# A decoder layer on one core: the low parts of the input projections' weights made by ACT and an adding DMA instead of DVE

## The chip, the cores and the metric

The kernel runs on one core of one Trainium2 chip. Its engines are TensorE (PE in the rows, with PEld its weight loads), VectorE (DVE), ScalarE (ACT) and GpSimd (POOL); SyncE (SP) issues most of the transfers. The metric is device time in microseconds, the median over runs; a profiled execution of the kernel is read beside it.

## The reference

One layer of a hybrid decoder on 512 prompt tokens and 8 x 4 decode tokens, d_model 1024: a half-step SwiGLU block, a mixer, a second half-step SwiGLU block, a gated per-layer embedding, and a final RMSNorm. All is in fp32. The mixer is where the change lies:

```python
proj = (h @ w_in).astype(f32)          # h: normed x, one combined input projection
z, xbc, dt_raw, q, fr, iv, og = jnp.split(proj, points, axis=-1)
# xbc: short convolution of width 4, then SiLU, gives xs, B, C (1536 columns)
y, new_ssm = _ssd_chunked(xs, dt, a, bm, cm, ssm0)        # 16 Mamba-2 heads, chunks of 128
y = y + d_skip[:, None] * xs                               # then * silu(z), norm
f = lb + (1.0 - lb) * jax.nn.sigmoid(fr)
o, new_hg = _gla_chunked(silu(q), 1.0 - f, iv, log(f), hg0)  # 8 HGRN2 heads, chunks of 16
o = rmsnorm(o) * hg_norm * silu(og)
mixed = concatenate([y_ssd, o]) @ w_out
```

## The kernel before

**Tiling.** Activations are kept transposed, 128 partitions by 544 columns (512 prompt and 32 decode tokens), and are read in two halves of 272 columns. The matmuls of the dense projections keep nearly fp32 precision with a faster format: every fp32 weight and activation is split into a high part, rounded to fp32r, and a low part, which is the rest (value minus high part). `mm6` forms a product as hi·xhi + hi·xlo + lo·xhi: per block of 128 input rows six matmuls, the first two with (whi, xwh), the next two with (whi, xwl), and the last two with the low part of the weight, (wlo, xwh).

**One projection.** `proj(src)` (L745) makes 128 columns of the input projection. `slab(src)` (L132) loads 512 KB of weights into `wraw` (two buffers, issued by SP, L138), lets ACT round it into `whi` (`cp`, L81; three buffers) and DVE make `wlo` = wraw − whi (`tt`, L69; three buffers). Then PE runs 8 x 6 = 48 matmuls (L84) into `ps_in`. Since the order in a block is whi, whi, whi, whi, wlo, wlo, the fifth matmul is the first that reads `wlo`. `proj` is called 52 times: 12 times for the convolution's columns (the loop over m), 32 times for the four projections of each of the 8 HGRN2 heads (f, q, v, og), and 8 times for z, the last two of them after the heads. The 16 slabs of the output projection w_out and others also go through `slab`; they are loaded by the same three buffers.

**Stages.** The first SwiGLU block ends at about 392 us of the span, and the first matmul of an input projection starts at 392.67. The 12 convolution projections run to about 515 us; there one projection follows the other on PE. Then the heads: per head h the code calls v of head h, f and q of head h+1 and og of head h, and puts between them the head's small matmuls: `attend` (pairs of decays, L1070 and others), `outs` (state updates, the decode states L1100), `finish`, and the stages of one chunk of the Mamba heads (`ssd_chunk` by `unit()`: L896 transposes of `cT`, then L943 and L946, which make y from `E`, `xdt` and `yk`, and a DVE row L72 that adds them into `cT`). `ps_s` are the small PSUM buffers (four), `ps_in` the large (two). The gates of a head (L994, L995, two scans on DVE) come from f. A head takes some 36 us; the z projections and the tail follow until about 843 us.

**Order.** In this stage the code of before and of the change leaves the order on each engine to a scheduler that builds the program; each engine then runs its own list in order, and waits at a row for what it reads, or for a buffer to come free. A DMA issued by POOL or SP likewise stands in that engine's list.

Of the kernel before, what the change touches and what calls it, by code (L numbers as in the profile page):

```python
# [9 lines left out]
F32 = mybir.dt.float32  # L10
F32R = mybir.dt.float32r
BF16 = mybir.dt.bfloat16
AF = mybir.ActivationFunctionType
ALU = mybir.AluOpType
# [3 lines left out]
P = 128  # L18
# [30 lines left out]
def body(ctx, tc, xT, pT, hconv, hssm, hhg, vecs, csts, w1u, w1d, w_in, w_dt, w_o, w2u, w2d, w_pg, w_pp,  # L49
         y_o, conv_o, ssmp_o, hgp_o, ssms_o, hgs_o):  # L50
    nc = tc.nc
    V, A, G, PE = nc.vector, nc.scalar, nc.gpsimd, nc.tensor

    def after(ins, prev):
        if prev is not None:
            tc.add_manual_dep(ins.ins, prev.ins.name,
                              mybir.DependencyInfo(mybir.DependencyClass.NoSync, mybir.DependencyReason.DATA),
                              reason="issue order")
# [3 lines left out]
    def pin(ins):  # L62
        if pinned[0]:
            after(ins, chain.get(ins.ins.engine))
            chain[ins.ins.engine] = ins
        return ins

    def tt(out, a, b, op, eng=None):
        pin((eng or V).tensor_tensor(out=out, in0=a, in1=b, op=op))  # L69
# [10 lines left out]
    def cp(out, a):  # L80
        pin(A.copy(out, a))  # L81
# [6 lines left out]
    def act(out, in_, f, scale=1.0, bias=0.0, **kw):  # L88
        ins = pin(A.activation(out=out, in_=in_, func=f, scale=scale, bias=bias, **kw))  # L89
        if tabled[1] and f not in (AF.Copy, AF.Square):  # L90
            after(ins, tabled[0])
            tabled[0] = ins

    def f32(t):
        return t.bitcast(F32)
# [3 lines left out]
    wp = ctx.enter_context(tc.tile_pool(name="wp", bufs=3))  # L99
# [32 lines left out]
    def slab(src, n=KD, parts=1):  # L132
        raw = wp.tile([P, 8, P], F32, name="wraw", tag="wraw", bufs=2)
        hi = wp.tile([P, 8, P], F32R, name="whi", tag="whi")
        lo = wp.tile([P, 8, P], F32R, name="wlo", tag="wlo")
        for i in range(parts):
            s = slice(i * n // parts, (i + 1) * n // parts)
            nc.sync.dma_start(raw[:, s], src[:, s])  # L138
            cp(hi[:, s], raw[:, s])
            tt(lo[:, s], raw[:, s], f32(hi[:, s]), ALU.subtract)  # L140
        return hi, lo
# [6 lines left out]
    def mm6(ps, whi, wlo, xhi, xlo, start, stop, m=P):  # L148
        seq = ((whi, xhi), (whi, xlo), (wlo, xhi))
        for n, (w, x) in enumerate(seq):  # L150
            for hf in range(2):
                mm(ps[:m, hf, :HN], w, x[:, hf * HN:(hf + 1) * HN], start=start and n == 0,
                          stop=stop and n == 2)
# [586 lines left out]
    with tc.tile_pool(name="ma", bufs=20, reuse_waits="tile") as ap:  # L740
# [2 lines left out]
            return ap.tile([P, T], dt, name=nm, tag="a")  # L743

        def proj(src):  # L745
            hi, lo = slab(src)
            ps = big.tile([P, 2, 512], F32, name="ps_in", tag="big")
            for k in range(KD):
                mm6(ps, hi[:, k], lo[:, k], xw[k][0], xw[k][1], k == 0, k == KD - 1)
            return ps  # L750

        cT = [ring(f"cT{m}") for m in range(12)]
        with ExitStack() as mix:
# [87 lines left out]
            for m in range(12):  # L841
                ps = proj(w_in[m])
                if m in (1, 3, 6, 8):
                    next(dtg, None)
                cin = sp.tile([P, SO + 7 * NB], F32, name="cin", bufs=2)
                G.memset(cin[:, 0:3], 0.0)
                smp = cin[:, SO:].rearrange("p (b t) -> p b t", t=7)
                G.tensor_copy(smp[:, :, 0:3], hist[:, m].rearrange("p (b t) -> p b t", t=3))
                tt(cin[:, 3:3 + HN], ps[:, 0, :HN], r[:, :HN], ALU.mult)
                tt(cin[:, 3 + HN:SO], ps[:, 1, :TP - HN], r[:, HN:TP], ALU.mult)  # L850
                tt(smp[:, :, 3:7], ps[:, 1, TP - HN:HN].rearrange("p (b t) -> p b t", t=4),
                   r[:, TP:].rearrange("p (b t) -> p b t", t=4), ALU.mult)
                G.tensor_copy(ncv[:, m, 0:3], cin[:, SO - 3:SO])
                G.tensor_copy(ncv[:, m, 3:27].rearrange("p (b t) -> p b t", t=3), smp[:, :, 4:7])
                L = SO + 7 * NB - 3
                ca = sp.tile([P, SO + 7 * NB], F32, name="ca", bufs=2)
                ts(ca[:, :L], cin[:, 0:L], vc("conv_w", m), ALU.mult, vc("conv_b", m), ALU.add)
                for j in range(1, 4):
                    stt(ca[:, :L], cin[:, j:j + L], vc("conv_w", 12 * j + m), ca[:, :L], ALU.mult, ALU.add)
                act(cT[m][:, :TP], ca[:, :TP], AF.Silu)  # L860
                act(cT[m][:, TP:].rearrange("p (b t) -> p b t", t=4),
                    ca[:, SO:].rearrange("p (b t) -> p b t", t=7)[:, :, 0:4], AF.Silu)
# [107 lines left out]
            def ev(h, i, nm):  # L970
                ps = proj(w_in[20 + 4 * h + i])
                t = hp.tile([P, T], F32, name=nm, tag=nm, bufs=1)
                tt(h2(t), ps[:, :, :HN], h2(r), ALU.mult)
                return t

            def zv(m, nm):
                ps = proj(w_in[12 + m])
                t = hp.tile([P, T], F32, name=nm, tag=nm, bufs=1)
                tt(h2(t), ps[:, :, :HN], h2(r), ALU.mult)
                return t  # L980
# [198 lines left out]
        with tc.tile_pool(name="mx", bufs=1, reuse_waits="tile") as xp:  # L1179
            mo = []  # L1180
            for k in range(8):
                hi = xp.tile([P, T], F32R, name="ohh", tag="ohl", bufs=16)
                lo = xp.tile([P, T], F32R, name="ohl", tag="ohl", bufs=16)
# [36 lines left out]
            for i, (m, h) in enumerate(halves):  # L1220
# [3 lines left out]
                hi, lo = slab(w_o[m, :, 8 - 8 * h:16 - 8 * h])  # L1224
# [21 lines left out]
    with tc.tile_pool(name="f3", bufs=34, reuse_waits="tile") as fp:  # L1246
# [3 lines left out]
        def eslot(nm, dt=F32):  # L1250
            return fp.tile([P, T], dt, name=nm, tag="e", bufs=12)
# [3 lines left out]
        for k in range(2):  # L1255
            t = eslot("pt")
            nc.sync.dma_start(t, pT[k])
            hi, lo = eslot("pth", F32R), eslot("ptl", F32R)
# [3 lines left out]
        for m in range(KD):  # L1262
            hi, lo = wpp[m // 4]
# [67 lines left out]
        for hf in range(2):  # L1331
# [3 lines left out]
            for m in range(KD):  # L1335
                if hf == 0 and m >= 2:
                    gslab(m)
                hi, lo = wg[m]
# [135 lines left out]
```

## Time and profile before

| | us |
|---|---|
| median of 2 runs | 1418.51 (1417.12 to 1419.89) |
| the profiled execution | 1418.97 |
| its span | 1417.2 |
| PE busy, of the span | 1384.7 (98%) |
| DVE busy | 1000.6 (71%) |
| ACT busy | 684.3 (48%) |
| POOL busy | 268.8 (19%) |

The profiled execution's own time is 1.8 us above its span. The mean granted TensorE clock is 0.98 of full speed. Busy time says how long an engine ran instructions; whether it sets the end is read from the idle time of the engine that is full, PE, and from what released it. Times in the rows are us from the span's start.

### The profile page before, as it was taken

Reading aid. Unit: us, or ns where it says so; the run is one execution under the profiler, and the core shown is the slowest. Engines: PE = TensorE matmul, PEld = TensorE weight load, DVE = VectorE, ACT = ScalarE, POOL = GpSimd, SP = SyncE. Lnnn points to the kernel's source line nnn. Section 1 sums busy time; section 2 is a strip of 40 time slices with the busy share of each in tenths; the row PEclk is TensorE's granted clock in tenths of the full one; section 3 lists DMA queues with packets and bytes.
Section 4 is the critical chain, followed back from the end, with each engine's and each line's share of the span. In section 5 each row is a group of like instructions: output and inputs, shape, how many; then the busy total and the mean of one; then the engine's idle time right before and its main releaser. Section 6 shows DMA issues by size and latency. Waiting matters only on the chain.

```text
span 1417.2 us, 27123 instructions
## 1 busy us (share of the span) xinstructions
PE 1384.7 (98%) x11069; PEld 1342.9 (95%) x11069; DVE 1000.6 (71%) x1603; ACT 684.3 (48%) x1232; POOL 268.8 (19%) x245
## 2 busy tenths in 40 slices
PE   7999999999999999999999999999899999999997
PEld 7999999999999999999999799999899999999896
DVE  6696666666568887777776577566877777776465
ACT  6544444443444365555553375455444444443655
POOL 0133332232111100000001021101333333320200
PEclk9999999999999999999999999999999999999898
DMA  6133233332432422222222445551344443334311
GB/s 228 43 93 105 90 90 94 100 95 73 149 111 77 139 93 93 93 93 93 93 100 72 140 152 172 187 170 46 107 120 125 128 137 120 119 101 116 105 45 64
DMA packets 67901, 154.99 MB, mean 109 GB/s; under 512 B 8576, under 2 KB 15872, under 8 KB 67776
## 3 DMA queue, kind: packets, MB, share of 16 engines
q1 hardware_dynamic: 66192, 150.65, 33.7%
q10 hardware_dynamic: 1584, 2.61, 0.5%
q8 instruction: 87, 1.43, 0.4%
q14 instruction: 38, 0.31, 0.1%
HBM read 138.70 MB, written 14.52 MB: 108 GB/s over the span
## 4 chain that ended last, share of the span: by engine, by line
PE 92%; DVE 4%; ACT 2%; issue 1%; DMA 0%; SPq 0%; DVEq 0%; ACTq 0%
PE ps_in L84 22%; PE ps_s L84 19%; PE ps_dn L84 19%; PE ps_ed L84 10%; PE ps_wo L84 6%; PE ps_up L84 4%; PE ps_s L1344 3%; PE ps_e L84 1%; PE ps_s L946 1%; PE ps_s L943 1%; PE ps_pg L1344 1%; DVE wlo L69 1%; DVE raw L69 1%; ACT whi L81 1%; PE ps_s L1056 1%
## 5 line engine op out<-in xcount | busy, mean ns | idle before, releaser
L81 ACT CAST whi<-wraw 128x1024 fp32r<-128x1024 f32 (+2 forms) x140 | 132.2, 950 | 200.5 <-PE ps_in L84 88.8
L69 DVE TENSOR_TENSOR wlo<-wraw,whi 128x1024 fp32r<-128x1024 f32 (+2 forms) x140 | 156.9, 1125 | 82.5 <-ACT whi L81 78.5
L84 PE MATMUL ps_in<-xwh,whi 128*128 128x272 f32 x832 | 183.6, 297 | 0.0
L84 PE MATMUL ps_in<-xwh,wlo 128*128 128x272 f32 x832 | 175.5, 291 | 0.0
L84 PE MATMUL ps_in<-xwl,whi 128*128 128x272 f32 x832 | 173.6, 289 | 0.0
L84 PEld LDWEIGHTS ps_in<-xwh,whi 128*128 128x128 f32 x832 | 132.4, 188 | 8.5 <-issue 8.2
L81 ACT COPY s<-ps_s 128x272 f32<-128x272 f32 x108 | 41.5, 384 | 195.5 <-PE ps_s L84 195.5
L84 PEld LDWEIGHTS ps_in<-xwh,wlo 128*128 128x128 f32 x832 | 130.7, 189 | 2.9 <-issue 2.9
L84 PEld LDWEIGHTS ps_in<-xwl,whi 128*128 128x128 f32 x832 | 131.1, 189 | 1.5 <-issue 1.5
L84 PE MATMUL ps_dn<-hl,dh 128*128 128x272 f32 x512 | 106.0, 288 | 2.5 <-DVE hl L69 2.5
L84 PE MATMUL ps_dn<-hh,dh 128*128 128x272 f32 x512 | 106.2, 289 | 0.0
L84 PE MATMUL ps_dn<-hh,dl 128*128 128x272 f32 x512 | 105.8, 288 | 0.0
L69 POOL TENSOR_TENSOR wraw<-r,r 128x512 f32<-128x512 f32 x36 | 48.7, 1353 | 263.4 <-DVE r L69 263.4
L84 PE MATMUL ps_s<-bx,w3h 128*128 128x272 f32 x576 | 85.2, 291 | 3.5 <-ACT s L81 3.5
L84 PEld LDWEIGHTS ps_dn<-hl,dh 128*128 128x128 f32 x512 | 80.5, 188 | 3.0 <-DVE hl L69 3.0
L84 PEld LDWEIGHTS ps_s<-bx,w3h 128*128 128x128 f32 x576 | 77.6, 191 | 3.9 <-ACT s L81 3.9
L84 PEld LDWEIGHTS ps_dn<-hh,dl 128*128 128x128 f32 x512 | 80.3, 188 | 0.2 <-DVE dl L69 0.2
L84 PEld LDWEIGHTS ps_dn<-hh,dh 128*128 128x128 f32 x512 | 80.4, 189 | 0.0
L69 POOL TENSOR_TENSOR g<-g,r 128x544 f32<-128x544 f32 x36 | 64.7, 1797 | 57.3 <-ACT g L89 56.0
L89 ACT ACT_TABLE_LOAD x55 | 70.6, 1283 | 4.4 <-DVE g L69 3.2
L69 DVE TENSOR_TENSOR w3l<-r,w3h 128x1024 fp32r<-128x1024 f32 x38 | 46.8, 1230 | 34.7 <-ACT w3h L81 34.7
L69 POOL TENSOR_TENSOR r<-r,wraw 128x512 f32<-128x512 f32 x36 | 49.2, 1366 | 103.4 <-DMA wraw<-in_w2u 54.8
(385 smaller groups left out, 3579.0 us busy)
## 6 DMA issues: line engine op xcount, KB each, us to landing
wraw<-in_w_in SPq DMA_DIRECT2D x52, 512.0 KB, 3.3
r<-in_w1u SPq DMA_DIRECT2D x22, 512.0 KB, 4.6
r<-in_w2u SPq DMA_DIRECT2D x22, 512.0 KB, 4.8
dr<-in_w1d SPq DMA_DIRECT2D x32, 256.0 KB, 3.3
h<-in_hssm SPq DMA_DIRECT2D x32, 256.0 KB, 4.1
wraw<-in_w_o SPq DMA_DIRECT2D x16, 512.0 KB, 4.2
dr<-in_w2d SPq DMA_DIRECT2D x32, 256.0 KB, 3.6
r<-in_w1u SPq DMA_DIRECT2D x18, 256.0 KB, 3.1
```

Of the source, the lines that this page charges most:

```text
L69: pin((eng or V).tensor_tensor(out=out, in0=a, in1=b, op=op))
L81: pin(A.copy(out, a))
L84: pin(PE.matmul(out, w, x, **kw))
L89: ins = pin(A.activation(out=out, in_=in_, func=f, scale=scale, bias=bias, **kw))
L943: PE.matmul(py[64 * e:64 * e + 64, q * P:q * P + n], xdt[:n, 2 * q + e], E[:n, 2 * q + e, :n], start=True, stop=pi is None, tile_position= ...
L946: PE.matmul(py[:, q * P:q * P + n], yf[:, q * P:(q + 1) * P], cs("sel") if smpl else cs("ident"), start=False, stop=True)
L1056: PE.matmul(pat[32 * j:32 * j + 32, c * P:(c + 1) * P], cw[:, c * P + 32 * j:c * P + 32 * j + 32], qs, start=True, stop=True, tile_positio ...
L1344: PE.matmul(ps[:, :HN], w[k // 4][:, k % 4 * P:k % 4 * P + P], xw[k][x][:, sl], start=k == 0 and n == 0, stop=k == KD - 1 and n == 2)
```

## The change

Only `proj` changes. The raw load and the high part stay, the latter now called directly on ACT. The low part is made in two steps: ACT writes the negative of the high part into `wlo` (Copy with scale −1), and then a DMA, issued by POOL, reads the same weights from HBM a second time and adds them in place onto `wlo`. The DVE subtraction is gone in 52 of the places where it stood. Nothing changes for the slabs of the output projection. Lines behind L745 stand 6 lower in the file of the change.

```diff
         def proj(src):
-            hi, lo = slab(src)
+            raw = wp.tile([P, 8, P], F32, name="wraw", tag="wraw", bufs=2)
+            hi = wp.tile([P, 8, P], F32R, name="whi", tag="whi")
+            lo = wp.tile([P, 8, P], F32R, name="wlo", tag="wlo")
+            nc.sync.dma_start(raw, src)
+            A.copy(hi, raw)
+            act(lo, f32(hi), AF.Copy, scale=-1.0)
+            G.dma_start(lo, src, accum_op=ALU.add)
             ps = big.tile([P, 2, 512], F32, name="ps_in", tag="big")
```

The order of the rows on the engines changes with it. On ACT, in a head, around the og projection (`Bk` is a copy for a Mamba chunk, `E` its decays, `ss` the head's norm). Before:

```order
L904 COPY Bk<-ps_s 128x128
L81 CAST whi<-wraw 128x1024
L89 ACTIVATE E<-E 128x1024
L89 ACT_TABLE_LOAD
L89 ACTIVATE ss<-ss,epsc 128x5
L81 CAST whi<-wraw 128x1024
L89 ACT_TABLE_LOAD
L89 ACTIVATE f<-f 128x544
```

and with the change:

```order
L910 COPY Bk<-ps_s 128x128
L750 CAST whi<-wraw 128x1024
L89 ACTIVATE E<-E 128x1024
L89 ACT_TABLE_LOAD
L89 ACTIVATE ss<-ss,epsc 128x5
L89 ACTIVATE wlo<-whi 128x1024
L750 CAST whi<-wraw 128x1024
L89 ACT_TABLE_LOAD
L89 ACTIVATE f<-f 128x544
L89 ACTIVATE wlo<-whi 128x1024
```

The negated copy does not stand right behind its cast: for og it stands behind `E`, a table load and `ss`, for the next v behind a table load and the sigmoid of f.

On POOL, in the convolution stage (`cin`, `ncv` and `hist` hold the convolution's history). Before:

```order
L846 MEMSET cin 128x3
L848 COPY cin<-hist 128x8x3
L853 COPY ncv<-cin 128x3
L854 COPY ncv<-cin 128x24
L846 MEMSET cin 128x3
```

and with the change:

```order
L859 COPY ncv<-cin 128x3
L860 COPY ncv<-cin 128x24
L752 DMA wlo<-in_w_in 128x1024
L852 MEMSET cin 128x3
L854 COPY cin<-hist 128x8x3
```

POOL's list now holds the adding DMA behind the two `ncv` copies of an earlier projection.

On PE, in `outs` of a head (`qm` and `s_` belong to the decode states, `E`, `xdt` and `yk` to the Mamba chunk, `ps_in` rows to a projection). Before:

```order
L1100 MATMUL ps_s<-s_7803,qm 32x128 x8
L84 MATMUL ps_in<-xwh,whi 128x272
L943 MATMUL ps_s<-E,xdt 64x128 x2
L946 MATMUL ps_s<-cst,yk 128x128
L84 MATMUL ps_in<-xwl,whi 128x272 x2
L84 MATMUL ps_in<-xwh,wlo 128x272 x2
L896 MATMUL ps_s<-cst,cT_4585 128x128
L896 MATMUL ps_s<-cst,cT_4586 128x128
L943 MATMUL ps_s<-E,xdt 64x128 x2
```

and with the change:

```order
L1106 MATMUL ps_s<-s_7837,qm 32x128 x8
L949 MATMUL ps_s<-E,xdt 64x128 x2
L952 MATMUL ps_s<-cst,yk 128x128
L84 MATMUL ps_in<-xwh,whi 128x272
L84 MATMUL ps_in<-xwl,whi 128x272 x2
L84 MATMUL ps_in<-xwh,wlo 128x272 x2
L84 MATMUL ps_in<-xwh,whi 128x272 x2
L84 MATMUL ps_in<-xwl,whi 128x272
L949 MATMUL ps_s<-E,xdt 64x128 x2
```

The pairs L943 (now L949) stand among other rows of the projection; six `ps_in` matmuls that stood ahead of this place in the pairs of `attend` now stand here and behind.

On DVE at the same place (`ass` belongs to the decode states; `f`, `cw` and `bb` to the gates, where `cw` and `bb` are the scans; `cT` the sums into the Mamba outputs). Before:

```order
L69 TENSOR_TENSOR wlo<-wraw,whi 128x1024
L72 SCALAR_TENSOR_TENSOR S<-S,dcs_71,ps_s 128x128 x3
L78 TENSOR_SCALAR f<-f 128x544
L69 TENSOR_TENSOR ass<-ps_s,cst 32x32
L994 SCALAR_TENSOR_TENSOR cw<-smask,lf 128x544
L72 SCALAR_TENSOR_TENSOR cT_4581<-cT_4581,vec,ps_s 128x128
L995 SCALAR_TENSOR_TENSOR bb<-smask,lf 128x544
L997 COPY mid<-cw 128x16
L69 TENSOR_TENSOR cb<-ps_s,cst 128x128
L72 SCALAR_TENSOR_TENSOR cT_4582<-cT_4582,vec,ps_s 128x128
```

and with the change:

```order
L72 SCALAR_TENSOR_TENSOR S<-S,dcs_71,ps_s 128x128 x3
L69 TENSOR_TENSOR ass<-ps_s,cst 32x32
L72 SCALAR_TENSOR_TENSOR cT_4581<-cT_4581,vec,ps_s 128x128
L78 TENSOR_SCALAR f<-f 128x544
L1000 SCALAR_TENSOR_TENSOR cw<-smask,lf 128x544
L1001 SCALAR_TENSOR_TENSOR bb<-smask,lf 128x544
L72 SCALAR_TENSOR_TENSOR cT_4582<-cT_4582,vec,ps_s 128x128
```

The subtraction that stood first is gone, and the second `cT` sum, which stood behind one scan and two short rows, now stands behind `f` and both scans.

## Rows read from the trace of the kernel before

**Rows 1.** First part of the page: busy time, share of the span, instructions
```profile
PE 1384.7 (98%) x11069; PEld 1342.9 (95%) x11069; DVE 1000.6 (71%) x1603; ACT 684.3 (48%) x1232; POOL 268.8 (19%) x245
```

**Rows 2.** Stretches: window, length; PE, PEld, DVE, ACT, POOL busy; clock, DMA share, GB/s
```profile
395.00:515.00 120.00, 120.00 (x978) 117.55 (x977) 91.91 (x182) 51.37 (x84) 17.90 (x55) 1.00 0.31 101
515.00:545.00 30.00, 29.83 (x277) 27.17 (x277) 26.07 (x57) 19.41 (x38) 1.87 (x2) 1.00 0.27 92
545.00:582.00 37.00, 36.84 (x328) 33.70 (x328) 28.55 (x61) 19.38 (x38) 1.86 (x2) 1.00 0.31 103
618.00:655.00 37.00, 37.00 (x329) 33.69 (x328) 28.75 (x61) 19.30 (x38) 1.86 (x2) 1.00 0.27 89
802.00:843.00 41.00, 40.22 (x305) 35.26 (x303) 30.54 (x52) 28.28 (x43) 12.42 (x8) 1.00 0.48 154
```

**Rows 3.** Groups by line, 393 to 843 us, DVE: busy, mean ns; idle before
```profile
L69 DVE TENSOR_TENSOR wlo<-wraw,whi 128x1024 fp32r<-128x1024 f32 x53 | 64.8, 1222 | 4.1 <-PE ps_in L84 2.9 <-ACT whi L81 0.3
```

**Rows 4.** DMA issues: tile, queue, count, size of one, median us to landing
```profile
wraw<-in_w_in SPq DMA_DIRECT2D x52, 512.0 KB, 3.3
```

**Rows 5.** Timeline of ACT, first and seventh projection: start, duration, row, wait
```profile
383.36 1.05 ACT L81 CAST whi<-wraw 128x1024 fp32r<-128x1024 f32 x1 [1.87 <-issue]
385.35 0.64 ACT L89 ACTIVATE sq<-x 128x544 f32<-128x544 f32 x1
423.77 1.03 ACT L81 CAST whi<-wraw 128x1024 fp32r<-128x1024 f32 x1
```

**Rows 6.** Timeline of ACT in one head, 640 to 677 us
```profile
644.73 0.66 ACT L89 ACTIVATE f<-f 128x544 f32<-128x544 f32 x1
651.09 0.65 ACT L89 ACTIVATE sg<-q 128x544 f32<-128x544 f32 x1
664.90 0.19 ACT L89 ACTIVATION_READ_ACCUMULATOR on<-ps_s 128x1 f32 x1
672.81 1.05 ACT L81 CAST whi<-wraw 128x1024 fp32r<-128x1024 f32 x1 [2.04 <-PE ps_in L84]
673.82 1.06 ACT L89 ACTIVATE E<-E 128x1024 f32<-128x1024 f32 x1
676.19 0.30 ACT L89 ACTIVATE ss<-ss,epsc 128x5 f32<-128x5 f32 x1
```

**Rows 7.** The chain that ended last, PE: start, length, matmuls of a projection
```profile
392.67 3.98 PE ps_in L84 x31
424.30 18.24 PE ps_in L84 x144
653.15 6.00 PE ps_in L84 x48
669.88 9.16 PE ps_in L84 x73
679.59 6.01 PE ps_in L84 x48
689.61 6.00 PE ps_in L84 x48
```

**Rows 8.** Timeline of SP and POOL
```profile
624.86 0.33 SPq L138 DMA_DIRECT2D wraw<-in_w_in  x1
425.27 0.20 POOL L854 COPY ncv<-cin 128x24 f32<-128x24 f32 x1
660.75 1.76 POOL L69 TENSOR_TENSOR og<-og,sg 128x544 f32<-128x544 f32 x1 [18.74 <-ACT sg L89]
```

**Rows 9.** Waits, 393 to 843 us: who waits <- for whom: total us, times, longest
```profile
PEld ps_s L943 <- DVE cT L72: 1.6, 7, 0.4
```

**Rows 10.** Timeline of DVE and PE in outs of one head
```profile
626.20 0.45 DVE L78 TENSOR_SCALAR f<-f 128x544 f32<-128x544 f32 x1 [0.19 <-ACT lf L89]
628.10 1.27 DVE L995 TENSOR_TENSOR_SCAN bb<-smask,lf 128x544 f32<-128x544 bf16 x1
629.57 0.33 DVE L72 SCALAR_TENSOR_TENSOR cT<-cT,vec,ps_s 128x128 f32<-128x128 f32 x1
630.06 0.44 PE L943 MATMUL ps_s<-E,xdt 128*64 128x128 f32 x4
635.63 1.66 DVE L78 TENSOR_SCALAR E<-E,acs 128x128 f32<-128x128 f32 x8 [0.34 <-DMA E<-acs_d]
```

## The prediction

> **What bounds the kernel now.** I read the busy times first, then the stretches of the stage that the change touches, then the chain, and at last the timelines of single engines around one projection. PE is busy 98% of the span, DVE 71%, ACT 48%, POOL 19% [rows 1]. The input projections lie between 393 and 843 us, and there PE is fuller still: 120.00 of 120.00 us in the convolution stretch, 37.00 of 37.00 in a head. The places with idle PE are 30.00−29.83 = 0.17, 37.00−36.84 = 0.16 and 41.00−40.22 = 0.78 us, together 1.1 us [rows 2]. So whatever DVE loses here, at most 1.1 us can be gained. The reader should not take DVE's 28.75 us of 37 in a head [rows 2] for a limit. The chain shows the same: 144 projection matmuls in 18.24 us with nothing between, so 6.08 us for each projection of the convolution stretch; 6.00 us in a head [rows 7].
>
> Hence the question is not what the 52 subtractions cost, but whether the new way to `wlo` is still ready in time.
>
> **What is removed.** The DVE subtraction takes 1.22 us, 64.8 us over the stretch [rows 3] (its 53rd belongs to the output projection). It lies beside full PE: worth nothing.
>
> **What is added on ACT.** One negated copy of 128x1024 per projection. No such row exists before; the cast of the same shape takes 1.05 and an ACT pass over `E`, same size, 1.06 [rows 6]. I take 1.06, so 52 × 1.06 = 55 us on an engine that is busy 19.30 of 37 us in a head and 51.37 of 120 in the convolution [rows 2]. It is hidden as long as `wlo` is in time.
>
> **What is added on the path of the weights: the adding DMA.** Call D the time from the end of the negated copy to the landed sum. The trace has no adding DMA and none of this size from POOL. Lower bound: the plain load of the same 512 KB by SP, 3.3 us [rows 4]. Upper bound for a DMA that works as these rows let expect: read the source, read the old `wlo`, write it, each a full landing, and the longest ordinary POOL row ahead of it in the list: 3 × 3.3 + 1.8 = 11.7 [rows 4, 8]. I take two landings and an issue of 0.33 us like SP's [rows 4, 8], 2 × 3.3 + 0.33 ≈ 7, as the nearest row is a single landing and the sum needs a second read.
>
> The Trainium skill ("DMA: Bandwidth & Descriptors", section "Anatomy of one DMA — SWDGE (gpsimd) path") gives a POOL-issued DMA about 2 us plus its bytes over 436 GB/s, an estimate of 3.2 us for 512 KB without an addition. By that price the sum below would lose its first term, 0.9 us.
>
> How much room is there? A cast starts when PE ends the projection three before, since there are three buffers. The room runs from the end of the negated copy to the fifth matmul, 0.5 us into the projection:
> - First projection: cast from 383.36, then the `sq` row that stands ahead of the new copy ends at 385.99 [rows 5], copy to 387.05; PE starts at 392.67 [rows 7], so 393.17 − 387.05 = 6.1 us.
> - Convolution, seventh: cast ends 424.80 [rows 5], copy 425.86; POOL's `ncv` copy ahead of the DMA has ended at 425.47 [rows 8]. PE starts it two projections after 424.30, at 436.46 [rows 7]: room 11.1. In steady state three projections take cast 1.05, copy 1.06, D, and 5.58 us from the first read of `wlo` to the projection's end, so the period is (7.68 + D)/3 where that is above 6.08: D over 10.6.
> - og: the copy stands behind `E` and `ss`, which ends at 676.49 [rows 6]; copy to 677.55, og starts at 689.61 [rows 7]: room 12.6.
> - v: behind the sigmoid of f (645.39) [rows 6], copy to 646.45; v starts when og ends, 653.15 + 6.00 = 659.15 [rows 7]: 13.2.
> - f: behind `sg` (651.74) [rows 6], copy to 652.80; f is the last 48 of the 73 matmuls from 669.88 and starts at 669.88 + 9.16 − 6.0 = 673.04 [rows 7]: 20.7.
> - q: behind the reads of the accumulators (665.09) [rows 6], copy to 666.15; q starts at 679.59 [rows 7]: 13.9.
>
> POOL's own rows ahead of the DMA, such as og's product, 1.76 us at 660.75 [rows 8], end before ACT's copy. With D = 7 only the first projection is late: 7 − 6.1 = **+0.9 us** (0 at D = 3.3; at 11.7, 5.6, and then the convolution adds ((7.68 + 11.7)/3 − 6.08) × 8 = 3). The heads: **0**.
>
> **What the new order moves.** In `outs` six projection matmuls that stood ahead now stand at or behind the `L943` pairs, so PE comes to the third pair 6 × 0.125 = 0.75 us earlier (6.00 us for 48 [rows 7]). That pair already waits for DVE's `cT` row, 7 times in the stretch and up to 0.4 us [rows 9]: the row runs from 629.57, PE's from 630.06 [rows 10]. In the new order the `cT` row stands behind `f` and both scans. `f` began at 626.20 as soon as ACT's `lf` was there, so it can't begin earlier; 626.20 + 0.45 + 2 × 1.27 = 629.19 [rows 10], 0.38 earlier than now, where the subtraction's 1.22 us gone would let hope for more. PE then waits 0.75 − 0.38 = 0.37 us more per head, and nothing else is in its list to fill it: 7 × 0.37 = **+2.6 us** (0 if DVE keeps up, 0.75 × 8 = 6.0 if it gains nothing).
>
> **Sum.** 1418.97 (the profiled execution, span 1417.2 and 1.8 around it; it lies 0.46 above the median of 1418.51) + 0.9 + 2.6 = **1422.5 us**. The ends of this case: −1.1 with no cost, 1417.9; +5.6 + 3 + 6.0, 1433.6.
>
> **Rivals.**
> *A. The adding DMA is far slower than plain ones, and PE waits for it (slower).* Its place: the first projection, every convolution projection from the fourth on, og in every head. In a head each us above 12.6 is paid once, as og stalls and everything behind shifts; 8 heads. At D = 20, six plain landings: first 13.9; convolution (27.68/3 − 6.08) × 8 = 25; heads 7.4 × 8 = 59; with the 2.6 together 101, so about **1520 us**. It costs 2% (28 us) from D ≈ 13.7: 7.6 + 8.3 + 8.8 + 2.6 = 27. For it: no row shows a DMA that adds, nor POOL writing one of 512 KB; the mixed step reads, converts and adds. Against it: 13.7 is four landings of 3.3 us, and the DMA engines are busy only 0.27 to 0.31 of the time in these stretches [rows 2], 0.48 in the last.
>
> *B. POOL is held up by DVE while it writes the transfer.* The stretch shows DVE busy 28.75 of 37 us [rows 2]. The longest unbroken piece named here is the run of eight `E` rows, 1.66 us [rows 10]; delayed by that, D is 8.7 and only the first projection pays 1.7 more. If all the DVE work within one projection's share of a head, 28.75/4 = 7.2 us, counted, D is 14.2: first 8.1, convolution 1.21 × 8 = 9.7, heads 1.6 × 8 = 13, with 2.6 together 33, so **1452 us**. For it: DVE and POOL were never asked for this at once; against it: DVE is idle a fifth of the time and its rows are short. The Trainium skill ("SBUF — State Buffer", section "SBUF: two separate sides") says that DVE's two-port operations shut POOL out so that the descriptors of its DMAs come late; no run here shows it yet. By that page the change loses, by the row of 1.66 us it does not.
>
> *C. DVE's relief makes it faster.* DVE is the second busiest engine, and 64.8 us leave it. But PE's idle time in the stretch is 1.1 us [rows 2]; even all of it gives **1417.9 us**, no gain of 2%. A larger one would need PE's rows themselves to run faster, at a clock that is 1.00 already [rows 2].
>
> **How the numbers follow.** Hidden, as in the sum: 0.67. D between 11.7 and 13.7, up to 1447 us: 0.06. A beyond that: 0.20. B at its higher price: 0.05. Faster than 2%: 0.02. About 2% is what a measurement of this kernel can tell from no change, so: faster 0.02, same 0.67 + 0.06 = 0.73, slower 0.20 + 0.05 = 0.25. The range: below, 1416, a little under the full gain of 1.1 us. Above it must take in B and the near part of A: 1470 is D ≈ 15.7 by the sum of A (9.6 + 13.7 + 25 + 2.6 = 51). What lies above it I give 0.15, below it 0.03. The hidden case's own range is 1417.9 to 1433.6.
>
> **What would show it.** In the profile after: DVE's `wlo` rows gone except those of the output projection; 52 new ACT rows of about 1.06 us; a DMA group from POOL, whose median landing is D without the wait in the queue (7 here; right up to about 11, wrong above 13.7). PE's weight loads waiting for a DMA: none but near 392 us if I am right; in the convolution stretch with a period above 6.08 and at og of each head if A is. If the heads keep 36.5 us (689.61 − 653.15 [rows 7]) and the `L949` waits for `cT` grow from 1.6 us to about 4, the order term is right. Long gaps between the end of the negated copy and the start of the DMA's packets, beside DVE rows, would show B. The prediction is wrong if D is above 13.7, or if the stretch gets shorter by more than 1.1 us.

## The result and the profile after

The changed kernel takes 1428.95 us (median, 1427.78 to 1430.13), against 1418.51 before: ratio 1.0086, 95% interval 1.0057 to 1.0114. That is slower by a little less than one per cent, within the 2% for which the word "same" was used, and inside the predicted range; the predicted time was 1422.5 us. The profiled execution spans 1428.3 us, 11.1 more than that of before. The direction and the case (the adding DMA is hidden) were right; some 6.5 us were missing from the sum, which had put 3.5 us on top of the time before where 10.4 came.

First part of the page, after: busy time, share, instructions. It answers to [rows 1].

```profile
PE 1382.3 (97%) x11069; PEld 1338.2 (94%) x11069; DVE 947.0 (66%) x1551; ACT 736.4 (52%) x1284; POOL 302.6 (21%) x297
```

DVE lost 53.6 us, ACT gained 52.1, and PE does the same work. The stretches that answer to [rows 2], in the same columns (the windows are cut by time, so a later row shows a slightly earlier point of the program than it did before):

```profile
395.00:515.00 120.00, 119.20 (x968) 116.52 (x968) 73.16 (x160) 68.56 (x100) 23.65 (x73) 1.00 0.76 183
515.00:545.00 30.00, 28.15 (x266) 25.79 (x265) 20.59 (x51) 22.12 (x41) 4.05 (x5) 1.00 0.61 146
545.00:582.00 37.00, 35.34 (x314) 32.12 (x313) 22.95 (x55) 23.96 (x44) 4.90 (x6) 1.00 0.63 151
618.00:655.00 37.00, 36.08 (x318) 32.86 (x314) 23.56 (x55) 22.80 (x42) 4.90 (x6) 1.00 0.59 144
802.00:843.00 41.00, 39.62 (x293) 33.22 (x292) 27.56 (x46) 22.37 (x31) 11.76 (x9) 1.00 0.63 184
```

PE, which had no gap in a head, now idles 37.00 − 36.08 = 0.92 us in one. Over all windows from 395 to 843 us the idle time rises from 1.1 to 10.4 us. The last two columns are the other thing to see: in the convolution stretch the bytes per second rose 1.8-fold (101 to 183 GB/s), but the DMA share 2.5-fold (0.31 to 0.76).

Who ended PE's waits, 393 to 855 us (engine, row that waits, releaser: total us, times, longest; PE's own idle time, and PEld where only the weight load waited):

```profile
PE ps_s L1120 <- DVE on L69: 3.9, 4, 1.7
PE ps_s L925 <- DMA h<-in_hssm: 2.8, 2, 1.5
PE ps_s L949 <- DVE cT L72: 2.4, 5, 0.5
PEld ps_s L949 <- DVE cT L72: 4.4, 8, 0.7
DVE E L78 <- DMA E<-acs_d: 17.1, 10, 4.5
```

Before, the waits for `on` and `h` were not there at all, and the wait for `cT` was 1.6 us at the weight loads [rows 9] and 0.3 us at PE itself. The last line is not PE's, but it is the key to the first. In the kernel before (393 to 845 us) the two read:

```profile
PE ps_s L943 <- DVE cT L72: 0.3, 2, 0.2
DVE E L78 <- DMA E<-acs_d: 2.1, 5, 0.7
```

Of DVE's 17.1 us the longest wait, 4.5, is for the first `E`, at 485 us, and PE has no idle time there; the others lie behind 515 us. The landings, 515 to 766 us. Of the kernel before:

```profile
E<-acs_d SPq DMA_DIRECT2D x7, 512.0 KB, 3.6
```

and of the changed one:

```profile
wraw<-in_w_in SPq DMA_DIRECT2D x28, 512.0 KB, 3.3
wlo<-in_w_in POOLq DMA_DIRECT2D x27, 512.0 KB, 5.4
E<-acs_d SPq DMA_DIRECT2D x7, 512.0 KB, 4.7
```

So the new path itself is fast enough, 5.4 us, but another transfer, `E`, lands 1.1 us later. What a late `E` does is seen in one head after the change, on DVE and PE in order of time:

```profile
526.60 0.71 DVE L69 TENSOR_TENSOR bb<-bb,f 128x544 f32<-128x544 f32 x1
529.27 1.77 DVE L78 TENSOR_SCALAR E<-E,acs 128x128 f32<-128x128 f32 x8 [1.95 <-DMA E<-acs_d]
530.84 0.68 DVE L69 TENSOR_TENSOR xde<-xdt,dend 128x512 f32<-128x512 f32 x1
535.08 0.68 DVE L69 TENSOR_TENSOR on<-ps_s,ss 128x512 f32<-128x512 f32 x1
535.91 0.63 PE L1120 MATMUL ps_s<-cst,on 128*128 128x128 f32 x4 [1.73 <-DVE on L69]
```

DVE has nothing to do for 1.95 us because `E` isn't there; behind `E` stand `xde`, `v`, three `qp` rows, the product of `E` with `cb`, a reciprocal and `on`, with no gap between them; PE has come to the transposes of `on` and waits 1.73 us. DVE is 66% busy and not the bound, and the place where it waits still reaches PE.

### The profile page after: what moved, and what is told of

It is laid out like the page before. It is cut to its first block, busy times and chain, and to the rows that moved or that the text cites. A ratio compares the mean times of both kernels' runs of the same rounds, so it can differ in the third digit from the quotient of the medians.

```text
span 1428.3 us, 27244 instructions
## 1 busy us (share of the span) xinstructions
PE 1382.3 (97%) x11069; PEld 1338.2 (94%) x11069; DVE 947.0 (66%) x1551; ACT 736.4 (52%) x1284; POOL 302.6 (21%) x297
## 4 chain that ended last, share of the span: by engine, by line
PE 86%; DVE 7%; DMA 3%; ACT 2%; issue 2%; SPq 0%; POOL 0%; DVEq 0%; ACTq 0%; POOLq 0%
PE ps_s L84 19%; PE ps_dn L84 18%; PE ps_in L84 17%; PE ps_ed L84 10%; PE ps_wo L84 6%; PE ps_up L84 3%; PE ps_s L1350 3%; DMA E<-acs_d 1%; DVE wlo L69 1%; PE ps_e L84 1%; PE ps_pg L1350 1%; PE ps_s L949 1%; DVE raw L69 1%; DMA h<-in_hssm 1%; PE ps_s L952 1%
## 5 line engine op out<-in xcount | busy, mean ns | idle before, releaser
L84 PE MATMUL ps_in<-xwl,whi 128*128 128x272 f32 x832 | 176.6, 291 | 0.0
L69 DVE TENSOR_TENSOR wlo<-wraw,whi 128x1024 fp32r<-128x1024 f32 (+2 forms) x88 | 93.5, 1069 | 80.8 <-ACT whi L81 80.4
L750 ACT CAST whi<-wraw 128x1024 fp32r<-128x1024 f32 x52 | 54.4, 1047 | 130.0 <-PE ps_in L84 126.2
L81 ACT CAST whi<-wraw 128x1024 fp32r<-128x1024 f32 (+2 forms) x88 | 77.8, 893 | 53.5 <-PE ps_dn L84 22.9
L752 POOL DMA_DIRECT2D wlo<-in_w_in x52 | 45.1, 868 | 243.8 <-ACT wlo L89 239.1
```

Of the source, the lines that this page charges most:

```text
L84: pin(PE.matmul(out, w, x, **kw))
L750: A.copy(hi, raw)
L752: G.dma_start(lo, src, accum_op=ALU.add)
```

## The experiments

Two theories stood against each other. **Theory 1:** the bytes of the adding DMAs make other transfers late, above all `E`, then `h` in the tail; the new order of the rows costs a further 3 us. **Theory 2:** the loss comes from the order and ACT's extra copies alone. Ratios are to runs of the kernel before on the same chip; differences to the changed kernel's 1428.95 us, which was measured at another time and only twice, are less sure.

A second measure is taken from the traces: the stretch from the first to the last matmul of an input projection, in which PE has the same 3699 rows in every run. It is 435.8 us before and 447.6 in the changed kernel, and is called the stage below. What stands ahead of it and behind it, and isn't touched, differs between these executions by 2 and 5 us.

### The adding DMA cut to an eighth

```diff
-            G.dma_start(lo, src, accum_op=ALU.add)
+            G.dma_start(lo[:, 0:1], src[:, 0:1], accum_op=ALU.add)
```

> The changed kernel with the adding DMA cut to the first of the eight blocks of a slab (64 KB of 512); the low parts of the other seven blocks stay the negated high part, so that product is left incomplete. Each engine's order of rows is that of the changed kernel; only the bytes moved are fewer. Theory 1 (the adding DMAs' traffic makes other transfers late: E of the Mamba chunks, then the normalised on in each head, and the states h in the tail): the landing of E goes from 4.7 back to about 3.6 us, DVE's waits for E from 17 to about 2 us, PE's idle time before L1120 (3.9) and L925 (2.8) and the first projection's 0.8 vanish, so about 1421.5 us (1428.95 - 7.5); the waits of the L949 rows for cT (4.4) stay, as they belong to the order. Theory 2 (the new order and ACT's extra copies make the loss, the DMA does not): all waits stay, 1427.5 to 1429.

Measured: 1420.34 us, ratio 1.0020 (1.0006 to 1.0034). The landing of `E` is 3.5 us again. PE's groups with idle time, 389 to 960 us (busy, mean ns, idle before and by whom):

```profile
L949 PE MATMUL ps_s<-E,xdt 128*64 128x128 f32 (+1 forms) x160 | 16.5, 284 | 2.7 <-DVE cT L72 2.6
L925 PE MATMUL ps_s<-h,Cm 128*32 128x512 f32 x32 | 9.7, 605 | 1.1 <-DMA h<-in_hssm 1.1
L1120 PE MATMUL ps_s<-cst,on 128*128 128x128 f32 x32 | 4.9, 275 | 0.4 <-DVE on L69 0.3
```

Every engine still runs the changed kernel's list, with ACT's copies and the POOL issues, and 8.6 of the 10.4 us between the two medians are not there; the stage takes 440.0 us, so 7.6 of 11.8 are gone. Theory 2 falls. What is left, 3.1 us over the kernel before in medians and 4.2 in the stage, is for the most part the wait for `cT`, which is unchanged; but the wait for `h` has not vanished, as theory 1 expected: 1.1 of 2.8 us are still there.

### Overwriting instead of adding

```diff
-            G.dma_start(lo, src, accum_op=ALU.add)
+            G.dma_start(lo, src)
```

> The changed kernel with the POOL DMA writing the weights over the negated copy instead of adding (the low part is then the whole weight, so the product is another one). Order on every engine as in the changed kernel, the same 512 KB read and written. Theory 1: if the addition itself costs the engines of the DMA their time, the landing falls from 5.5 us to about 3.3 + 0.9 and the DMA's busy share in the convolution stretch from 0.76 to about 0.6, E lands near 4.0 us, and the time lies between, 1423 to 1426 us. If only the second read of 512 KB matters, landing and share stay and the time is 1428 to 1430. Theory 2 (order and ACT): 1427.5 to 1429, whatever the landing does.

Measured: 1427.24 us, ratio 1.0066 (1.0044 to 1.0087); the interval overlaps that of the changed kernel, so a gain of the whole is not shown. The price of adding is read from the queue instead. POOL's queue, 395 to 515 us (packets, MB, share of the 16 DMA engines), without the addition:

```profile
q0 software_dynamic: 2602, 9.47, 26.0%
wlo<-in_w_in POOLq DMA_DIRECT2D x18, 512.0 KB, 4.3
```

and of the changed kernel:

```profile
q0 software_dynamic: 2628, 9.53, 46.3%
wlo<-in_w_in POOLq DMA_DIRECT2D x18, 512.0 KB, 5.6
```

For the same bytes the adding packets hold the DMA engines 1.8 times as long, and land 1.3 us later (in the heads 5.4 against 3.7). But `E` lands at 4.7 us in both (medians), and PE's idle time before the transposes falls from 3.9 to 1.9 us, where the addition of an eighth left 0.3; that for `h` is 1.9, between 2.8 and 1.1. The stage takes 443.4 us, between 447.6 and 440.0. So in the traces a second stream of 512 KB without the addition does about half of the harm, and in the medians, 1427.24 against 1420.34 and 1428.95, most of it; the runs don't settle the share. As expected, the landing and the share of the DMA engines took a middle value; the landing of `E` (4.0 expected) and the median did not.

### Two buffers for E

```diff
-                E = sp.tile([P, 8, P], F32, name="E", bufs=1)
+                E = sp.tile([P, 8, P], F32, name="E", bufs=2)
```

> The changed kernel with two buffers for E instead of one, so that E's load of the next Mamba chunk needn't wait until PE has read the last one. Theory 1 (a late E holds DVE's list, behind which stand v, qp and on): DVE's waits for E fall from 17 us to below 3, PE's idle time before L1120 from 3.9 to below 0.5 us, and the time by 3 to 5 us, to about 1425 us. Theory 2 (order and ACT): on is late for another reason, the L1120 waits stay and the time is 1427.5 to 1429.

Measured: 1424.46 us, ratio 1.0043 (1.0031 to 1.0056). No idle time of PE before the transposes of `on` is listed any more, and DVE waits for `E` only at the end of the convolution stretch:

```profile
DVE E L78 <- DMA E<-acs_d: 5.4, 2, 5.1
```

`E` itself lands later than ever, 5.2 us. So it is not the lateness as such that costs, but that one buffer lets its load start only when PE has read the last `E`. With the second buffer the scheduler also moved DVE's rows on the next `E` from before `on` to behind it, as in one head of this kernel:

```profile
568.83 0.69 DVE L69 TENSOR_TENSOR on<-ps_s,ss 128x512 f32<-128x512 f32 x1
571.23 1.27 DVE L78 TENSOR_SCALAR E<-E,acs 128x128 f32<-128x128 f32 x6
```

So the run takes both the wait and these rows of 1.66 us out of the way of `on`, and doesn't part the two. The wait for `h` fell as well, from 2.8 to 1.1 us. The gain, 4.5 us in medians and 5.4 in the stage (442.1 us), is that of all this together; PE's idle time puts 3.9 of it on `on`.

### The adding DMA twice

```diff
             G.dma_start(lo, src, accum_op=ALU.add)
+            G.dma_start(lo, src, accum_op=ALU.add)
```

> The changed kernel with the adding DMA issued twice, one after the other, into the same low part (the weights are added twice there, so the product is another one). The price D of the path doubles from about 6 to about 12 us, and the traffic of the additions too. If the rooms of the prediction hold (6.1 us at the first projection, 10.6 in the convolution stretch, 12.6 to 20.7 in the heads): first projection +6, convolution ((7.68 + 12)/3 - 6.08) x 8 = +4, heads 0 by the low parts themselves, and later landings of E and h, about as much again as now (+7): 1440 to 1450 us, with PE waiting for wlo in the convolution stretch alone. If the rooms are smaller than worked out by 3 us, the heads wait too: above 1465 us. If the traffic is harmless (theory 2): 1439 us.

Measured: 1520.50 us, ratio 1.0729 (1.0693 to 1.0766), 70 us beyond what I expected. The price of the path did not double, it went to about 20 us. POOL in the convolution stretch:

```profile
435.20 0.86 POOL L753 DMA_DIRECT2D wlo<-in_w_in  x1 [7.41 <-DMA wlo<-in_w_in]
436.02 1.21 POOL L752 DMA_DIRECT2D wlo<-in_w_in  x1
443.48 0.88 POOL L753 DMA_DIRECT2D wlo<-in_w_in  x1 [6.00 <-DMA wlo<-in_w_in]
```

The second addition (L753) waits in POOL's list for the first to land, and blocks the next projection's first one (L752) behind it. The copy that ends at 429.14 gets its first addition at 436.02, its second at 443.48, and PE reads it at 449.1: D = 20 us. The formula of the prediction gives (7.68 + 20)/3 = 9.2 us for the period; PE's reads of `wlo` that had to wait lie at 440.47 and 475.77, four projections apart, so 8.8. But the period is set by POOL's list here: L753 follows L753 after 8.7 us on average (435.20 to 478.68, five projections), and POOL waits for nothing but landings in between. With three low parts under way, D then follows from the period as much as the period from D, so the formula agrees and is not tested as a cause. What is seen of rival A is that late low parts stop PE. Its sum is not borne out: of the 43.1 us that PE waited for `wlo`, 7.8 lie at the first projection, 14.6 at the other eleven of the convolution and 20.7 at the forty that follow, where rival A has 13.9, 25 and 59. That the total of 1520 agrees is luck: here the transfers of `E` and `h` are late too (`on` 7.1, `cT` 8.1, `h` 4.3 us of idle PE), and the granted clock was 0.89 in the convolution stretch instead of 1.00, where PE sat idle 21 of 120 us.

### DVE adds, no second read

```diff
-            G.dma_start(lo, src, accum_op=ALU.add)
+            tt(lo, raw, f32(lo), ALU.add)
```

> ACT's negated copy as in the changed kernel, but DVE adds the raw weights to it (wlo = wlo + wraw) and no POOL DMA is issued: no second read. PE's order in the heads is that of the changed kernel (the same eight projection matmuls between the second and the third L949 pair), with 52 DVE additions of about 1.22 us back in DVE's list. Theory 1 (traffic 7 us and order 3 us): E lands after 3.6 us, no waits for L1120 and L925 beyond those of before, the cT waits at L949 remain 4 us or more since DVE's list is longer: 1419 to 1422 us, as with the adding DMA cut to an eighth (1420.34). Theory 2 (the loss lies in ACT's copies): 1427 us or more. If the order costs nothing: 1417 to 1418.

Measured: 1420.90 us, ratio 1.0030 (1.0019 to 1.0042). `E` lands at 3.7 us, nothing waits for `h` or `on` beyond 0.3 us, and the wait for `cT` is that of the changed kernel:

```profile
PEld ps_s L949 <- DVE cT L72: 4.7, 8, 0.7
```

This kernel shares with the changed one ACT's copies and PE's order in the heads, and has DVE's 52 rows back. It loses 4.2 us, and 3.3 in the stage (439.1 us); PE's own idle time for `cT` is 2.6 us in this trace and in that of the first experiment, 0.3 before. With that experiment (3.1 and 4.2 us) the order term comes to about 3 to 4 us. The two differ in DVE's load and agree in PE's list but for 70 of its 3699 rows. ACT's copies stand in both, so that they are not parted from the order; no idle time of PE in either trace ends with an ACT row.

### The traffic alone, onto the raw buffer

In `proj` of the kernel before, with `slab` written out there:

```diff
             nc.sync.dma_start(raw, src)
             cp(hi, raw)
             tt(lo, raw, f32(hi), ALU.subtract)
+            G.dma_start(raw, src, accum_op=ALU.add)
```

> The kernel before, with DVE's subtraction, and behind it a POOL DMA that adds the same 512 KB onto the raw weights' buffer once both have read it. Nobody reads the sum; all outputs come from the old path. PE's order in the heads is that of before. Theory 1: only the traffic is added, so E lands at about 4.7 us, PE waits before L1120 and L925 as in the changed kernel (3.9 and 2.8 us), the waits for cT stay at 1.6 and the first projection doesn't wait: 1418 + 6 to 7 = 1424 to 1425 us (a raw buffer that comes free later may add 1 or 2). If the loss needs the new order or the path of the low part: 1417 to 1419.

Measured: 1466.67 us, ratio 1.0351 (1.0333 to 1.0369). As a test of the traffic it failed: the raw buffer comes free only when the addition has landed, so the next load is late, and ACT's casts wait for it.

```profile
ACT whi L81 <- DMA wraw<-in_w_in: 51.5, 18, 7.0
```

### The new path in the convolution stretch alone

`proj` gets a flag; without it the low part comes from `slab` as before. The loop over the 12 convolution projections sets it, the heads and z don't:

```diff
-        def proj(src):
+        def proj(src, add):
+            if add:
...
+            else:
+                hi, lo = slab(src)
```

> The changed path in the 12 convolution projections alone; the heads and z make the low part on DVE as before. Theory 1: here the DMA share is highest (about 0.75) but no transfer that PE waits for is in the way, so only the first projection waits, 0.8 us, and the first E of the Mamba chunks may be late: 1418 to 1420 us. If the DMA engines' load by itself slows PE: above 1422.

Measured: 1417.24 us, ratio 1.0002 (0.9987 to 1.0017).

```profile
395.00:515.00 120.00, 120.00 (x978) 117.54 (x977) 83.74 (x173) 62.21 (x94) 20.59 (x65) 1.00 0.59 151
```

The share of 0.59 is a mean of two parts, for the 12 convolution projections end at about 476 us, not at 515 as the section on the kernel before has it; the other projections in this stretch belong to the heads. The part with the additions alone:

```profile
395.00:465.00 70.00, 70.00 (x559) 68.44 (x558) 43.44 (x103) 39.23 (x57) 16.22 (x57) 1.00 0.75 172
```

A DMA share of 0.75, against 0.27 before in the same window, costs nothing here: PE is full, and the stage takes 435.9 us. The last addition is issued at 459 us and has landed before the first load of `E` starts, at 482. The load of the DMA engines did no harm by itself; nor did every late transfer: POOL waited 6.2 us for `hist` here, 1.9 before, and PE didn't notice.

### The gates later, with the small DMA

```diff
-                unit()
-                if more:
-                    ga = gates(h + 1, f, q)
-                unit()
+                unit()
+                unit()
+                if more:
+                    ga = gates(h + 1, f, q)
```

> The changed kernel with the adding DMA cut to the first of eight blocks (so the low part is incomplete in the others), and the gates of the next head written behind the second of the two units, so that DVE's cT rows stand ahead of f and the scans. The same with the old place of the gates took 1420.34. The order theory: the waits of L949 for cT fall from 4.2 to below 1 us and the time by 2 to 3, to 1417.5 to 1418.5 us, that of before. If the 3 us are not those waits: 1420 to 1421 still. If the later gates make the next head's q and e late: a new wait before L1062 or L1074, above 1422.

Measured: 1435.47 us, ratio 1.0126 (1.0109 to 1.0143). The waits of L949 for `cT` are gone but for 0.2 us, and a larger one has come, before a projection that stands behind the norm's reciprocal `ss`:

```profile
PE ps_in L84 <- DVE ss L1114: 9.9, 7, 2.8
```

The granted clock fell to 0.96 in one head as well. So the wait for `cT` goes when the gates stand later; but the lists of PE and DVE moved at many other places too, and what the wait is worth isn't told by this run.

### The traffic alone, in the heads, onto a scratch tile

In `proj` of the kernel before, with a flag that the 32 projections of the heads set:

```diff
             hi, lo = slab(src)
+            if more:
+                sc = hp.tile([P, 8, P], F32R, name="wsc", bufs=2)
+                act(sc, f32(hi), AF.Copy, scale=-1.0)
+                G.dma_start(sc, src, accum_op=ALU.add)
```

> The kernel before with DVE's subtraction everywhere; in the 32 projections of the heads ACT also makes a negated copy in a scratch tile, and a POOL DMA adds the 512 KB of weights onto it. Nobody reads the scratch, so no path waits for it; PE's order is that of before. Theory 1 (the traffic alone delays E, then DVE's list, then on): E lands at 4.5 to 4.8 us instead of 3.6, DVE's waits for E go from 2 to above 8 us, PE waits before L1120; the waits at L949 stay at 1.6. Of the changed kernel's 11 us the heads' part without order and tail, so 2 to 5 us over the kernel before. If the traffic only hurts where the new order has thinned DVE's list: within 1 us of before.

Measured: 1431.08 us, ratio 1.0096 (1.0078 to 1.0115). `E` lands at 4.9 us, and the waits are those expected, with the order of before (L947 is L943 there, L1118 is L1114):

```profile
DVE E L78 <- DMA E<-acs_d: 12.4, 9, 2.8
PE ps_s L1118 <- DVE on L69: 3.4, 5, 1.3
PEld ps_s L947 <- DVE cT L72: 1.6, 7, 0.4
PE ps_s L927 <- ACT kk L1043: 5.7, 5, 1.8
ACT whi L81 <- DMA wraw<-in_w_in: 29.5, 6, 6.0
```

Nothing reads the scratch tile, PE's order is the old one but for 10 of 3699 rows, and PE waits for `on` all the same: it needs neither the new order nor the new path. The stream came with 32 more copies on ACT; in the first experiment ACT has 52 of them, and `on` was 0.3 us late in all. The last two lines show what I did not expect: here the raw load is late too (4.2 us to landing instead of 3.3), the cast waits for it, and `kk`, which stands behind the cast in ACT's list, reaches PE late. The total is therefore above the 2 to 5 us that I gave, and does not price the `E` chain by itself.

### The new path in the heads alone

Edit as for the convolution, with the flag set for the 32 projections of the heads.

> The changed path in the 32 projections of the heads alone; the 12 of the convolution stretch and the 8 of z make the low part on DVE as before. Theory 1: the order term (3 us, PE's order in the heads is the changed one) and the late E (about 4 us), without the late states h in the tail (2.8 us) and without the wait for wlo at 509 us (0.8): 1417 + 6 to 7.5 us. If the loss came from the convolution stretch or z: within 2 us of before.

Measured: 1425.94 us, ratio 1.0056 (1.0037 to 1.0076), 7.3 us over the kernel before in medians. PE's groups with idle time:

```profile
L952 PE MATMUL ps_s<-E,xdt 128*64 128x128 f32 (+1 forms) x160 | 16.5, 284 | 2.2 <-DVE cT L72 1.9
L1123 PE MATMUL ps_s<-cst,on 128*128 128x128 f32 x32 | 5.0, 278 | 6.0 <-DVE on L69 5.9
```

The heads hold two thirds or more of the loss: 7.3 of 10.4 us in medians, and in the stage 10.7 (446.5 us) of 11.8, of which some belongs to 3 us at a granted clock of about 0.5, which follow PE's first wait for `on`, 1.9 us. The wait for `h` has gone with the additions of z, that for `on` is larger than in the changed kernel, 5.9 against 3.9. The wait for `wlo` that I had put on the convolution is still there, 0.7 us at 510.9: it belongs to a projection of the heads. The total agrees with theory 1.

## Why the prediction was right or wrong, point by point

**What bounds the kernel: right.** 53.6 us less DVE brought nothing; with the new path in the convolution projections alone, where it costs nothing either, the time is that of before to 0.2%. So rival C is out.

**The price D: right in kind, 7 taken, about 5.8 measured.** The copies take 1.05 us. In the head at 640 to 680 us the POOL DMA starts 0.3 us after the copy's end and lands 5.4 to 5.6 us later. The prediction gave 7, and bounds of 3.3 and 11.7.

```profile
DMA to landing us min/median/max: 5.4/5.5/5.6
```

Over the whole kernel the landings go from 5.0 to 9.3 us, with 5.5 in the middle. Rival B has no support: of the 52 additions twelve ran beside a DVE busy 94% of the time or more, and eleven of these landed in 5.0 to 5.5 us, one in 6.5; the seven that took over 7 us ran beside a DVE busy 13 to 76%. Without the addition a POOL-issued DMA of this size landed in 3.7 to 4.3 us. The Trainium skill ("DMA: Bandwidth & Descriptors", section "Anatomy of one DMA — SWDGE (gpsimd) path") would give it an estimate of 3.2; the measurement is above that.

**First projection +0.9: wrong, it is 0.** D was smaller than the room of 6.1. The copy starts at 384.06 and the first matmul with `wlo` at 391.23, with no wait. The one wait for `wlo` is elsewhere, 0.8 us at 509.5, in a projection of the heads whose addition took 8.3 us to land; that it is nearly the size of the forecast term is luck.

```profile
384.06 1.05 ACT L89 ACTIVATE wlo<-whi 128x1024 fp32r<-128x1024 f32 x1
391.23 0.41 PE L84 MATMUL ps_in<-xwh,wlo 128*128 128x272 f32 x2
509.51 0.52 PE L84 MATMUL ps_in<-xwh,wlo 128*128 128x272 f32 x2 [0.80 <-DMA wlo<-in_w_in]
```

**Rooms in the convolution stretch and the heads: right.** No low part was late there but for that one.

**The order term of +2.6: right.** Predicted: the waits of L949 for `cT` grow from 1.6 to about 4. They are 4.4 us, the longest 0.7; PE's own idle time for `cT` grew from 0.3 to 2.4, so by 2.1. The two kernels with this order and little or no second read lose 3.1 and 4.2 us in medians.

**The step that failed: what stands beside the transfers was costed at nothing.** The prediction took the DMA engines' share of 0.27 to 0.31 [rows 2] as evidence that a second stream has room, and priced only the new transfer itself. It did not ask which transfers were already the last to arrive. The row was in hand: the `E` rows at 635.63 began 0.34 us late, ended by their DMA [rows 10]. Here 1.1 us more to the landing of `E` went straight into DVE's list, to `on` and to PE. The terms that were missing, as PE's idle time in the changed kernel: 3.9 us for `on`, 2.8 for `h`. The first experiment, which takes back most of the bytes and nothing else, returns 8.6 us; two buffers for `E` return 4.5. The measured time lies in the hidden case's own range, 1417.9 to 1433.6, but that range was made of D and the order term; that it holds the missing terms as well is luck.

**Rival A: not what happened, but its mechanism exists.** With the additions doubled, D was 20, the low parts came late, and PE waited for them 43 us, though less in the heads than rival A has it, and with POOL's list setting the pace.

**Left open.** The span grew by 11.1 us: the stage by 11.8 (435.8 to 447.6), what follows it by 1.2, while what stands ahead of it, which the change does not touch, was 1.9 shorter in this execution. Of the stage's 11.8 us 10.1 are idle time of PE, nearly all of it `on`, `h`, `cT` and the one `wlo`; the other 1.7 are a longer busy time of the same rows and were not followed, nor was why `h` still waits 1.1 us beside an eighth of the bytes. That the `cT` order alone makes the 3 us is argued from two kernels which share it; the run that moved the place put another wait there. No version faster than the kernel before was found, and 1.1 us is all that PE has to give in this stage.

## What to carry to other kernels

When a change adds a transfer, price it twice: whether it lands in time, and what it does to every transfer that someone already waits for; a wait that ends with the name of a DMA, however short, marks a chain to follow as far as the engine that bounds. Not every such wait reaches it: that of POOL for `hist` grew by 4.3 us in the run with the convolution alone and cost nothing. Work taken from an engine that is not the bound brings nothing, and here the scheduler spent the freed place on an order that costs. Harm comes at places, not by the average: the same extra stream cost nothing where no load of `E` stood beside it.

## What the runs showed of the hardware

A DMA that adds held the DMA engines 1.8 times as long as one that overwrites, 46.3% against 26.0% of the stretch for some 9.5 MB, though it landed only 1.3 to 1.7 us later. POOL's own row for one such issue takes 0.87 us, for the overwriting one 0.53, and stands in its list like any instruction; an issue that waits for an earlier landing blocks all of POOL's list, 6.0 to 7.4 us in the doubled kernel. In the heads, beside the additions, a load of 512 KB by another queue (`E`) landed in 4.7 us instead of 3.6, while the raw weights' load, of the same size, stayed at 3.3; it rose from 3.3 to 3.7 between 395 and 515 us, and to 4.2 in the heads of the run with the scratch tile. With the DMA engines busy 0.75 of the time PE ran 70.00 of 70.00 us in the convolution.
